# Weight and token sums of a seven-product MLP, made ahead and kept in DRAM

## The chip, the cores and the metric

The kernel runs on one core of a Trainium2 chip. The metric is the device time of one execution in microseconds, as a median of several executions. All data is float32. Each large matrix product is made of three TensorE passes over a high and a low part of both operands (below).

## What is computed

One decoder layer over 2048 tokens of width 1024: a mixer (retention heads beside pooling), cross-attention into 256 memory tokens, and a gated MLP, each with a residual, then a last RMSNorm. The change concerns the MLP, with D_FF = 2816:

```python
def conv_glu_ffn(h, w_up, conv_w, conv_b, w_down):
    a = h @ w_up
    ...
    c = conv_w[0] * a2 + conv_w[1] * a1 + conv_w[2] * a + conv_b
    gate, val = jnp.split(c, 2, axis=-1)
    return (jax.nn.silu(gate) * val) @ w_down
...
    for l in range(DEPTH):
        ...
        x = x + cross_attn(rmsnorm(x, xa_norm_g[l]), mem_n, xa_wq[l], xa_wkv[l], xa_wo[l])
        x = x + conv_glu_ffn(rmsnorm(x, ffn_norm_g[l]), ffn_w_up[l], ...)
    return rmsnorm(x, final_norm_g)
```

## The kernel before

Tokens lie along the free axis, features on the 128 partitions. The tokens are worked in two blocks of 1024 (index `b`), each of two halves of 512. A product of two float32 matrices is taken as high x high + high x low + low x high in a rounded format: `passes` (lines 227 to 229) issues the three matmuls of a weight tile and a token tile. The high part is a ScalarE copy, the low part a subtraction, mostly on VectorE (`low`, L894 and L202).

The program runs in stages. First the attention weights are folded together (`folded_weights`), beside loading of x; then, for each token block, values, four retention heads, four pooling groups, the mixed output with its residual, attention, and its output with the residual. All of these but the attention scores and the values are made of `unit`s: one weight tile of 512 KB, split into parts, against eight token tiles, 48 matmuls. Weights wait in `raws` (five places of 1024 columns in the tile R), split pairs in `prs` (three places in Q).

Then comes the MLP, for both blocks: two rounds of the up-projection (one for each block), then three rounds of the down-projection for block 0 and three for block 1. A round keeps one set of split token tiles in G, 7 x n tiles of 128 x 512, and takes its members against them. A member is a 2 x 2 block of weight tiles with a 2 x 2 block of token tiles, multiplied in seven products instead of eight (a scheme of sums, products and sums after). `Up` has n = 4 pairs per product, 22 members a block; `Down` has n = 3, 4 and 4, four members a round. Item i of a member is one product: 3n matmuls into one PSUM bank, followed by its evacuation on VectorE or ScalarE. For items 1, 2 and 5 the weight operand is a sum of tiles, which `Member.add` makes on GpSimd each time (four additions a member: the R<-R rows of GpSimd). For indices 1 to 4 the token operand is a difference, which `combining` makes on GpSimd (T<-T) from two loaded tiles of Hd (normalized tokens) or Gd (gated products). The letters in `how` say who makes the low part of each of the seven weight operands: "" is VectorE directly, "copy" ScalarE into PSUM and then VectorE, "pool" GpSimd.

Between two rounds the token tiles must be replaced in place: tile (i, j) of the next round can be written once the last member of this round has passed item i, and is wanted when the next round reaches it.

`run` writes the order of the MLP out by hand, item by item, with small queues (`pending`, `later`, `after`) for work that comes some items later. What it emits, and all of the stages before, then goes through the Tile scheduler, which simulates the engines and, on each, issues what is ready, earlier program rows first. Each engine and SP's queue of DMA issues carries out its own list in order on the chip.

Of the kernel before, what the change touches and what calls it, by code (L numbers as in the profile page):

```python
# [30 lines left out]
EDGE = 16  # L31

# [85 lines left out]
def trunk(ctx, tc, xT, memT, pos, w_qkgu, w_v, wkv, wqT, wo, wout_r, wout_p, poolT, w_up, w_dn, vecs, consts, outT):  # L118
# [55 lines left out]
    Hd = drp.tile([NB, KT, P, T], F32, tag="Hd", name="Hd")  # L174
    Gd = drp.tile([NB, NF, P, T], F32, tag="Gd", name="Gd")
# [87 lines left out]
    behind = [iter(())]  # L263
# [5 lines left out]
    def unit(raw, rhs, evac, order=range(4)):  # L269
# [4 lines left out]
        for h in range(2):  # L274
            for s in range(NS):
# [4 lines left out]
                next(behind[0], None)  # L280
                if h == 1:
                    evac(s, ps[s])
# [517 lines left out]
    def attention(sums, beside):  # L800
# [37 lines left out]
        for i in range(2 * KT):  # L838
# [22 lines left out]
            late = prob[hp], t, e  # L861
            next(more_m if i < KT - 2 else beside, None)
# [5 lines left out]


# [6 lines left out]
    class Round:  # L876


        def __init__(self, src, first, second, groups):
            self.src, self.first, self.second, self.groups = src, first, second, groups  # L880

            self.shared = False
            self.n = len(first)
            self.held = [None] * self.n
# [13 lines left out]
    def combining(rd, i, j):  # L898

        k1, k2 = rd.first[j], rd.second[j]  # L900
        r = q = None

        def load(k, s):
            r = TT.take()
            sp.dma_start(r.f[:, :SUB], rd.src(k, s))
            return r

        if i in (0, 5, 6):
            r = load(k1 if i == 0 else k2, 1 if i == 5 else 0)
        elif i in (1, 4):  # L910
            r = load(k1, 1)
            q = load(k2 if i == 1 else k1, 1 if i == 1 else 0)
        else:
            q = load(k1 if i == 2 else k2, 0)
        yield
        yield
        if i in (2, 3):
            r = rd.held[j]
        x = r.f[:, :SUB]
        if q is not None:  # L920
            a, b = (q, r) if i == 2 else (r, q)
            tt(pool, x, a.f[:, :SUB], b.f[:, :SUB], ALU.subtract)
            q.free()
            if i == 1:
                rd.held[j] = r
            yield
        hi, lo = right(i, j, 0), right(i, j, 1)
        act.activation(hi, x, AF.Copy)  # L928
        yield
        low(x, hi, lo, "pool" if rd.shared and (i * rd.n + j) % 3 == 2 else "copy" if i in (1, 2) else "")  # L930
        if i not in (1, 2):
            r.free()

    def in_turn(gens):

        live, gens = [], list(gens)
        while live or gens:
            if gens and TT.room() >= 2:
                live.append(gens.pop(0))
# [5 lines left out]
    class Member:  # L945


        def __init__(self, loads, halves):
            self.loads, self.n = loads, halves

            self.sign, self.how = 1, ("", "copy", "copy", "", "copy", "copy", "")
            self.raw = {}

        def fetch(self):

            g, h = ((0, 0), (1, 0), (1, 1), (0, 1))[len(self.raw)]
            w = self.n * P
            r = raws.take()
            sp.dma_start(r.f[:, :w], self.loads[g][:, h * w : (h + 1) * w])
            self.raw[g, h] = r  # L960

        def add(self, i):

            while len(self.raw) < (1, 2, 3, 3, 3, 4, 4)[i]:
                fetches.pop(0).fetch()
            w = self.n * P
            q = {k: r.f[:, :w] for k, r in self.raw.items()}
            a11, a12, a21, a22 = (q.get(k) for k in ((0, 0), (0, 1), (1, 0), (1, 1)))
            self.t = None
            if i == 1:  # L970
                self.t = H.take()
                x = self.t.f[:, :w]
                tt(pool, x, *((a11, a21) if self.sign > 0 else (a21, a11)), ALU.subtract)
            elif i == 2:

                tt(pool, a21, a21, a22, ALU.add)
# [670 lines left out]
```

## Time and profile before

| what | value |
|---|---|
| median of three executions | 2580.94 us (2580.14 to 2583.87) |
| profiled execution: its own time | 2577.88 us |
| profiled execution: its span | 2576.1 us |
| TensorE busy | 2468.0 us (96%) |
| VectorE / ScalarE / GpSimd busy | 1861.0 / 1246.6 / 816.4 us |
| DMA, mean over the span | 126 GB/s, 323.74 MB |

The time outside the span is 1.8 us in the profiled execution. In the span the stages before the MLP take about 1190 us, the two up-projection rounds until about 2060, the six down-projection rounds until about 2530, and the last norm the rest. A row of a group view gives line, engine, operation, output and input tiles with shapes, count, total busy time, mean of one, and the idle time before it with what ended it. One line number can be that of a helper: L202 is every two-operand operation of VectorE or GpSimd, so rows are told apart by tiles: G<-... and Q<-... are low parts of token and weight operands, Z<-... evacuations and convolution, R<-R weight sums, T<-T token sums.

### The profile page before, as it was taken

The page shows a single profiled execution, that of the slowest core. Times are in us where ns is not written, and L with a number is a line of the kernel's source. Part 1 is how long each engine was busy: PE and PEld are TensorE (multiplying, and loading weights), DVE is VectorE, ACT ScalarE, POOL GpSimd, SP SyncE. Part 2 cuts the span into 40 slices and gives each one's busy share as a digit, 9 for nine tenths or more (in the row PEclk, how much of TensorE's full clock was granted, in tenths as well). Part 3 has the DMA queues.
Part 4 walks back from the last instruction along what each step waited for, and adds up shares of the span by engine and source line. Part 5 has one row for each costly group of instructions (what it writes and reads, how often), then busy time and mean ns, then how long its engine had stood idle before and what let it go on. Part 6 is the DMA issues. An engine that isn't in the chain of part 4 may idle for free. (4 is left out here: it accounts for less than half of the span.)

```text
span 2576.1 us, 32736 instructions
## 1 busy us (share of the span) xinstructions
PE 2468.0 (96%) x11382; PEld 2045.6 (79%) x11382; DVE 1861.0 (72%) x2840; ACT 1246.6 (48%) x2240; POOL 816.4 (32%) x642
## 2 busy tenths in 40 slices
PE   7999999999999999998999999899999988989896
PEld 7888888888788888876788888688888866777675
DVE  8655564746736655435998888888888788888997
ACT  7334323534222234335555566555656574565654
POOL 0011130000301100014444445844444654543661
PEclk9999999999999999998999999899999999999998
DMA  8134424324311143144342223422222355548751
GB/s 289 49 101 141 132 83 150 115 90 141 137 33 41 35 142 119 40 169 155 106 160 98 86 94 131 147 82 86 84 89 90 136 179 184 188 165 266 252 168 70
DMA packets 166165, 323.74 MB, mean 126 GB/s; under 512 B 16752, under 2 KB 38896, under 8 KB 166000
## 3 DMA queue, kind: packets, MB, share of 16 engines
q1 hardware_dynamic: 140912, 292.29, 33.3%
q10 hardware_dynamic: 25088, 29.37, 3.3%
q8 instruction: 90, 1.47, 0.2%
q14 instruction: 75, 0.61, 0.1%
HBM read 249.76 MB, written 71.83 MB: 125 GB/s over the span
## 5 line engine op out<-in xcount | busy, mean ns | idle before, releaser
L227 PE MATMUL mm<-G,Q 128*128 128x512 f32 (+1 forms) x1944 | 755.8, 389 | 18.0 <-ACT Q L219 10.2
L228 PE MATMUL mm<-G,Q 128*128 128x512 f32 (+1 forms) x1944 | 750.1, 386 | 7.9 <-DVE G L202 7.9
L229 PE MATMUL mm<-G,Q 128*128 128x512 f32 (+1 forms) x1944 | 750.4, 386 | 7.0 <-DVE Q L202 6.9
L202 POOL TENSOR_TENSOR R<-R 128x512 f32<-128x512 f32 (+1 forms) x272 | 414.3, 1525 | 481.9 <-DMA R<-w_up 177.8
L227 PE MATMUL mm<-G 128*128 128x512 f32 (+1 forms) x1384 | 537.6, 389 | 20.4 <-DVE T L202 7.5
L228 PE MATMUL mm<-G 128*128 128x512 f32 (+1 forms) x1384 | 538.6, 389 | 16.4 <-DVE G L202 16.4
L229 PE MATMUL mm<-G 128*128 128x512 f32 (+1 forms) x1384 | 536.8, 388 | 0.0
L227 PEld LDWEIGHTS mm<-G,Q 128*128 128x128 f32 x1944 | 369.9, 190 | 91.3 <-ACT Q L219 10.6
L229 PEld LDWEIGHTS mm<-G,Q 128*128 128x128 f32 x1944 | 369.4, 190 | 82.2 <-DVE Q L202 9.6
L228 PEld LDWEIGHTS mm<-G,Q 128*128 128x128 f32 x1944 | 370.2, 190 | 80.0 <-DVE G L202 9.9
L227 PEld LDWEIGHTS mm<-G 128*128 128x128 f32 x1384 | 263.3, 190 | 77.6 <-DVE T L202 7.9
L228 PEld LDWEIGHTS mm<-G 128*128 128x128 f32 x1384 | 263.0, 190 | 75.0 <-DVE G L202 23.0
L229 PEld LDWEIGHTS mm<-G 128*128 128x128 f32 x1384 | 263.1, 190 | 52.1
L211 DVE SCALAR_TENSOR_TENSOR Z<-Z,vecs 128x1024 f32<-128x1024 f32 x176 | 254.0, 1443 | 69.8 <-ACT Z L1064 69.0
L202 DVE TENSOR_TENSOR Q<-R,Q 128x512 fp32r<-128x512 f32 (+1 forms) x234 | 175.8, 753 | 172.4 <-ACT Q L219 148.7
L202 POOL TENSOR_TENSOR T<-T 128x512 f32<-128x512 f32 (+3 forms) x140 | 203.7, 1465 | 279.3 <-PE mm L229 181.0
L202 DVE TENSOR_TENSOR Z<-Z,mm 128x512 f32<-128x512 f32 (+1 forms) x272 | 213.7, 786 | 28.7 <-PE mm L229 23.8
L894 ACT ACTIVATE aux<-R 128x512 f32<-128x512 f32 (+1 forms) x272 | 153.0, 580 | 152.6 <-POOL R L202 116.7
L202 POOL TENSOR_TENSOR Z<-Z,T 128x512 f32<-128x512 f32 x37 | 57.5, 1558 | 485.6 <-DVE T L202 398.1
L219 ACT ACTIVATE Q<-R 128x512 fp32r<-128x512 f32 x150 | 93.9, 628 | 237.1 <-PE mm L228 212.2
L928 ACT ACTIVATE G<-T 128x512 fp32r<-128x512 f32 x210 | 129.3, 628 | 155.7 <-POOL T L202 118.2
L202 DVE TENSOR_TENSOR G<-T,G 128x512 fp32r<-128x512 f32 (+1 forms) x211 | 173.2, 830 | 38.9 <-ACT G L219 18.7
(163 smaller groups left out, 2846.1 us busy)
## 6 DMA issues: line engine op xcount, KB each, us to landing
T<-Gd SPq DMA_DIRECT2D x198, 256.0 KB, 3.3
R<-w_up SPq DMA_DIRECT2D x176, 256.0 KB, 2.8
Gd<-Z SPq DMA_DIRECT2D x44, 512.0 KB, 2.6
T<-Hd SPq DMA_DIRECT2D x72, 256.0 KB, 3.1
R<-w_qkgu SPq DMA_DIRECT2D x32, 512.0 KB, 3.5
R<-w_dn SPq DMA_DIRECT2D x64, 256.0 KB, 3.3
T<-xT SPq DMA_DIRECT2D x48, 256.0 KB, 3.0
T<-Xd SPq DMA_DIRECT2D x48, 256.0 KB, 3.4
```

The costliest lines, as they stand in the source:

```text
L202: return eng.tensor_tensor(out=out, in0=a, in1=b, op=op)
L211: dve.scalar_tensor_tensor(out=out, in0=a, scalar=s, in1=b, op0=op0, op1=op1)
L219: act.activation(hi, src, AF.Copy)
L227: pe.matmul(ps, lh, rh, start=start, stop=False)
L228: pe.matmul(ps, lh, rl, start=False, stop=False)
L229: pe.matmul(ps, ll, rh, start=False, stop=stop)
L894: act.activation(t, x, AF.Copy)
L928: act.activation(hi, x, AF.Copy)
```

## The change

Four things are changed together.

Weights: a generator `weight_sums` makes, once for both blocks, the four sums of each member's weights (22 jobs for up, 12 for down) and keeps them in DRAM (`Ud`, `Dd`). It is stepped from `unit` and from the attention loop, and uses 2048 columns of R that `raws` gives up (three places instead of five). A member of the MLP then loads seven tiles instead of four and adds nothing.

Tokens: Hd and Gd hold ready-made operands, seven or eight per pair of tiles. Those of the normalized tokens are made where they are normalized (`normed_tiles`, `later_tiles`), those of the products when the second tile of a pair is done (`pair`: the first is loaded back, four GpSimd operations, four stores). `combining` loads one tile for each operand.

Low parts: `how` changes; for `Up` items 2 and 6 are GpSimd's and item 5 goes straight to VectorE; for `Down` items 2 and 6 are GpSimd's, 0, 1, 3 and 4 copied. Of the token low parts GpSimd does every third in rounds 1 and 2 as before, and now every fourth in the other rounds (`shared`).

The scheduler uses its detailed simulation (a timeline) in place of its usual one.

```diff
+ROUNDS = ((0, 3), (6, 4), (14, 4))
...
-    Hd = drp.tile([NB, KT, P, T], F32, tag="Hd", name="Hd")
-    Gd = drp.tile([NB, NF, P, T], F32, tag="Gd", name="Gd")
+    Hd = drp.tile([NB, KT // 2, 7, P, SUB], F32, tag="Hd", name="Hd")
+    Gd = drp.tile([NB, NF // 2, 8, P, SUB], F32, tag="Gd", name="Gd")
+    Ud = drp.tile([NF, 4, P, SUB], F32, tag="Ud", name="Ud")
+    Dd = drp.tile([len(ROUNDS), KT // 2, 4, P, SUB], F32, tag="Dd", name="Dd")
...
                 next(behind[0], None)
+                next(under[0], None)
...
+    def weight_sums(spare):
+        jobs = [((w_up[f], w_up[f + NF]), 0, 4, Ud[f], 1) for f in range(NF)]
+        for at, (k0, n) in enumerate(ROUNDS):
+            jobs += [((w_dn[2 * j], w_dn[2 * j + 1]), k0, n, Dd[at, j], -1) for j in range(KT // 2)]
+        for w, k0, n, to, sign in jobs:
+            q = [spare.take() for _ in range(4)]
+            a11, a12, a21, a22 = (r.f[:, : n * P] for r in q)
+            for i, a in enumerate((a11, a12, a21, a22)):
+                sp.dma_start(a, block(w, i // 2, i % 2, k0, n))
+            yield
+            yield
+            tt(pool, a22, a21, a22, ALU.add)
+            tt(pool, a21, *((a11, a21) if sign > 0 else (a21, a11)), ALU.subtract)
+            yield
+            tt(pool, a11, a22, a11, ALU.subtract)
+            tt(pool, a12, a12, a11, ALU.subtract)
+            yield
+            for i, a in enumerate((a21, a11, a22, a12)):
+                sp.dma_start(to[i][:, : n * P], a)
+            for r in q:
+                r.free()
+            yield
...
-        if q is not None:
-            a, b = (q, r) if i == 2 else (r, q)
-            tt(pool, x, a.f[:, :SUB], b.f[:, :SUB], ALU.subtract)
...
-        low(x, hi, lo, "pool" if rd.shared and (i * rd.n + j) % 3 == 2 else "copy" if i in (1, 2) else "")
+        low(x, hi, lo, "pool" if (i * rd.n + j) % rd.shared == rd.shared - 1 else "copy" if i in (1, 2) else "")
...
+    def sums_of(b11, b12, b21, b22, t):
+        tt(pool, t, b12, b22, ALU.subtract)
+        tt(pool, b12, b12, b11, ALU.subtract)
+        yield
+        tt(pool, b11, b11, t, ALU.subtract)
+        tt(pool, b21, b11, b21, ALU.subtract)
+        yield
...
+            own = [sums[i][:, : halves * P] for i in range(4)]
+            self.loads = [part(0, 0), own[0], own[1], part(1, 1), own[2], own[3], part(0, 1)]
...
-            self.b, self.f, self.how = b, f, ("", "copy", "copy", "", "copy", "copy", "pool")
+            self.b, self.f, self.how = b, f, ("", "copy", "pool", "", "copy", "", "pool")
...
+                def pair():
+                    if TT.room() < 3:
+                        after(1, pair)
+                        return
+                    x = [TT.take() for _ in range(3)]
+                    b11, b12, t = (r.f[:, :SUB] for r in x)
+                    sp.dma_start(b12, to[7])
+                    sp.dma_start(b11, to[0])
+                    todo = sums_of(b11, b12, one, two, t)
...
-            self.b, self.j, self.at, self.sign = b, j, at, -1
+            self.b, self.j, self.at, self.how = b, j, at, ("copy", "copy", "pool", "copy", "copy", "", "pool")
...
-        out[1].shared = out[2].shared = True
+        out[1].shared = out[2].shared = 3
...
+    raws = Places([(R, j * T) for j in range(3)], T)
+    under[0] = weight_sums(Places([(R, 3 * T + i * SUB) for i in range(4)], SUB))
...
-    with tile.TileContext(nc) as tc:
+    with tile.TileContext(nc, schedule_with_timeline_sim=True) as tc:
```

Where the order moves: SP's queue in the front, from the loads of the positions (`pos`) on. w_qkgu are the weights of the heads' units, wqT those of a folding step; w_up into R and R into Ud are the sums' loads and stores. Before:

```order
L531 DMA T<-pos 64x512 x2
L286 DMA R<-w_qkgu 128x1024 x2
L403 DMA R<-wqT 128x1024 x2
L286 DMA R<-w_qkgu 128x1024
L403 DMA R<-wqT 128x1024
L286 DMA R<-w_qkgu 128x1024 x2
```

and now, from the same loads:

```order
L536 DMA T<-pos 64x512 x2
L291 DMA R<-w_qkgu 128x1024
L408 DMA R<-wqT 128x1024
L889 DMA R<-w_up 128x512 x2
L899 DMA Ud<-R 128x512 x2
L889 DMA R<-w_up 128x512 x2
L899 DMA Ud<-R 128x512
L889 DMA R<-w_up 128x512 x2
L408 DMA R<-wqT 128x1024
L899 DMA Ud<-R 128x512 x3
```

The second wqT now stands behind six loads and three stores of sums, and the scheduler has drawn the jobs far ahead of the places where the program steps them: the loads of the last of the 34 stand before the sixth wout_r load of block 0. SP issues 1569 transfers in all, where it issued 953.

GpSimd's queue near the end of the down-projection. R<-R are weight sums, T<-T token sums; G<-R,G and G<-T,G are low parts of weight and token operands. Before:

```order
L202 TENSOR_TENSOR T<-T 128x512 x5
L202 TENSOR_TENSOR R<-R 128x512
L202 TENSOR_TENSOR T<-T 128x512
L202 TENSOR_TENSOR R<-R 128x512
L202 TENSOR_TENSOR T<-T 128x512 x4
```

and now:

```order
L206 TENSOR_TENSOR G<-T,G 128x512 x3
L206 TENSOR_TENSOR G<-R,G 128x512
L206 TENSOR_TENSOR G<-T,G 128x512
L206 TENSOR_TENSOR G<-R,G 128x512
L206 TENSOR_TENSOR G<-T,G 128x512
```

No sums are left on GpSimd there; what stands in their place are low parts that were VectorE's.

More of the change, by code (lines that the diff above doesn't have):

```diff
@@ L861, in attention @@
             late = prob[hp], t, e
+            next(under[0], None)
             next(more_m if i < KT - 2 else beside, None)
@@ L1257, in after, with until_room @@
         waiting.append((clock[0] + n, f))
+    def until_room(places, n):
+        for _ in range(99):
+            if places.room() >= n:
+                return
+            w = min(waiting, key=lambda w: w[0])
+            waiting.remove(w)
+            w[1]()
+        assert False, "no room"
     pending, later, sums, Y, fetches = [], [], [], [], []
@@ L1275, in run @@
         items = [(rd, g, m, i) for rd in rds for g in rd.groups for i in range(7) for m in g]
-        fetches[:] = [m for rd in rds for g in rd.groups for _ in range(4) for m in g]
-        made, added, highs = [], [], []
+        fetches[:] = [(m, i) for _, _, m, i in items]
+        made, highs = [], []
         tiles, due, live = [], [], []
@@ L1555, in trunk @@
     more()
+    for a in (state.rearrange("p h n -> p (h n)"), cs_t[:, P + 1 : P + 1 + SUB]):
+        TT.freed.append(len(TT.one))
+        TT.one.append(Arena(a, 0, 1, SUB))
     for r in xs:
```

227 lines of the change are left out of this document (112 added, 115 removed).

## The prediction

> **What bounds the kernel now.** I read the page's head, then busy time by stretches of the span, then TensorE's waits, then groups by form. The page:
>
> ```profile
> span 2576.1 us, 32736 instructions
> PE 2468.0 (96%) x11382; PEld 2045.6 (79%) x11382; DVE 1861.0 (72%) x2840; ACT 1246.6 (48%) x2240; POOL 816.4 (32%) x642
> ```
>
> The stretches; columns are stretch, length, then busy us and instructions of PE, PEld, DVE, ACT, POOL, then granted clock, DMA share, GB/s:
>
> ```profile
> 0.00:70.00 70.00, 54.50 (x402) 51.92 (x402) 61.09 (x104) 49.73 (x81) 6.29 (x9) 0.98 0.76 273
> 50.00:60.00 10.00, 6.82 (x44) 6.42 (x43) 8.96 (x13) 6.56 (x11) 0.00 (x0) 0.83 1.00 346
> 45.00:400.00 355.00, 349.19 (x1841) 299.81 (x1841) 218.47 (x434) 136.94 (x282) 45.46 (x42) 1.00 0.36 115
> 650.00:1175.00 525.00, 520.25 (x2489) 434.37 (x2489) 276.56 (x580) 152.43 (x332) 66.32 (x57) 1.00 0.26 89
> 1175.00:1275.00 100.00, 85.22 (x353) 67.77 (x352) 79.23 (x107) 54.43 (x91) 47.76 (x35) 0.91 0.38 128
> 1300.00:1600.00 300.00, 300.00 (x1326) 248.47 (x1325) 257.85 (x300) 178.45 (x279) 142.46 (x112) 1.00 0.31 109
> 1620.00:1680.00 60.00, 50.22 (x191) 39.10 (x190) 53.65 (x54) 35.18 (x59) 48.01 (x35) 0.89 0.40 133
> 2060.00:2520.00 460.00, 416.92 (x1747) 334.43 (x1746) 404.69 (x546) 278.89 (x516) 242.44 (x173) 0.96 0.59 197
> ```
>
> TensorE is the bound almost everywhere: in the middle of the first up-projection round it is busy 300 of 300 us and issues 1326 matmuls, 4.42 per us or 0.226 us each. Nothing done for the other engines there can pay. Counting matmuls against that rate shows where time is lost, the lowered clock included: entry to the up-projection (1175 to 1275) 353 of 442, so 89 / 4.42 = 20 us; change of token block (1620 to 1680) 191 of 265, 17 us; down-projection (2060 to 2520) 1747 of 2033, 65 us. The prize is at most these 102 us. Before them, 650 to 1175 loses under 5 us.
>
> Who is waited for there: TensorE's waits at the block change (first row) and from 2000 on (the others); columns are total us, times, longest.
>
> ```profile
> PE mm L228 <- DVE G L202: 8.1, 5, 2.4
> ...
> PE mm L228 <- DVE G L202: 16.3, 12, 4.1
> PE aux L296 <- DVE T L202: 12.3, 2, 9.9
> PE mm L227 <- DVE Z L202: 10.0, 9, 2.0
> ```
>
> G is the token operand, Z the accumulators: VectorE's low parts and evacuations come last. Beside them VectorE is busy 405 of 460 us (88%) in the down-projection. Its groups, then GpSimd's, from 2080 to 2510 (count | busy, mean ns | idle before):
>
> ```profile
> L202 DVE TENSOR_TENSOR G<-T,G 128x512 fp32r<-128x512 f32 x102 | 90.0, 896 | 5.7 <-ACT G L928 5.3
> L202 DVE TENSOR_TENSOR G<-aux,G 128x512 fp32r<-128x512 f32 x73 | 48.3, 682 | 9.8 <-ACT aux L894 5.6 <-ACT G L989 3.4
> L202 DVE TENSOR_TENSOR Q<-R,Q 128x512 fp32r<-128x512 f32 x23 | 19.3, 838 | 7.3 <-ACT Q L989 7.3
> L202 DVE TENSOR_TENSOR G<-R,G 128x512 fp32r<-128x512 f32 x21 | 19.2, 915 | 6.4 <-ACT G L989 6.3
> L202 DVE TENSOR_TENSOR G<-R,G 128x384 fp32r<-128x384 f32 x12 | 9.4, 779 | 0.5 <-ACT G L989 0.5
> L202 DVE TENSOR_TENSOR Q<-R,Q 128x384 fp32r<-128x384 f32 x10 | 6.6, 657 | 1.6 <-ACT Q L989 1.6
> ...
> L202 POOL TENSOR_TENSOR T<-T 128x512 f32<-128x512 f32 x76 | 109.2, 1450 | 55.5 <-DMA T<-Gd 43.7 <-ACT aux L894 6.9 <-issue 4.2
> L202 POOL TENSOR_TENSOR R<-R 128x512 f32<-128x512 f32 x62 | 91.0, 1472 | 105.5 <-DMA R<-w_dn 66.9 <-DVE Q L202 27.3 <-issue 6.9
> L202 POOL TENSOR_TENSOR R<-R 128x384 f32<-128x384 f32 x24 | 28.3, 1185 | 43.2 <-DMA R<-w_dn 21.4 <-DVE Q L202 8.6 <-issue 5.7
> ```
>
> The sums that the change takes away here are GpSimd's R and T rows. What helps VectorE is that GpSimd, freed of them, takes over low parts.
>
> **Down-projection, by steps.** A member is one pair of weight tiles. Its seven low parts were three direct VectorE ones and four through a ScalarE copy; now two are GpSimd's, one direct, four copied. Over 24 members VectorE loses 48 direct ones; the four R rows give (19.3 + 19.2 + 9.4 + 6.6) / 66 = 0.83 us, so 40 us. Of 154 token tiles GpSimd did 7 low parts (every third of one round of 21) and will do 40 (one round at every third, five at every fourth): 33 fewer, 5 in 7 at 0.90 and 2 in 7 at 0.68, so 28 us. GpSimd's stretch falls from 242 us to 32 x 1.47 + 16 x 1.19 + 40 x 1.47 = 125. The gap of 0.21 us between 896 and 682, which only operations with both inputs in SBUF show, should then halve: on some 170 such operations 17 us more. VectorE goes from 405 to about 320 us, while the 1747 matmuls need 395: 81%. In the steady up-projection it stands at 258 of 300, 86%, and TensorE loses nothing. So load ceases to be the limit; bursts at round changes and the 9.9 us wait of the statistics remain. I take 35 of the 65 us, with 10 and 60 as ends.
>
> On that gap the Trainium skill (SBUF — State Buffer, section Who interferes with whom) states an exclusive lock: with two SBUF inputs VectorE is fully blocked for as long as GpSimd's reading instruction holds the pair. By it an operation arriving at random against 53% occupancy by 1.45 us would wait 0.38 us, not the 0.21 shown, and the halving would be worth about 31 us instead of 17; the sum uses the row.
>
> **The two entries.** One token tile at the up-projection's start, engine by engine, in the timeline (start, length, instruction, idle before):
>
> ```profile
> 1198.21 1.29 POOL L202 TENSOR_TENSOR T<-T 128x512 f32<-128x512 f32 x1 [3.23 <-DMA T<-Hd]
> 1199.53 0.63 ACT L928 ACTIVATE G<-T 128x512 fp32r<-128x512 f32 x1 [1.81 <-POOL T L202]
> 1200.20 1.10 DVE L202 TENSOR_TENSOR G<-T,G 128x512 fp32r<-128x512 f32 x1 [2.22 <-ACT G L928]
> ...
> 1215.29 0.79 PE L227 MATMUL mm<-G 128*128 128x512 f32 x1 [7.51 <-DVE T L202]
> ```
>
> The tile arrives ready-made now: GpSimd's 1.3 us and the second load go, while ScalarE's and VectorE's steps stay. I take half of each loss: 10 (2 to 16) and 8 (0 to 14) us. At the block change GpSimd was 80% busy (48 of 60), which is the load removed.
>
> **Up-projection between them: nothing.** ScalarE loses 88 copies, VectorE 44 low parts. GpSimd loses 176 sums, gains 44 low parts and 88 sums of product tiles: per second-half tile 2 x 1.47 + 4 x 1.45 = 8.7 us and two short halo copies, of the 19 us that its 84 matmuls take. Three more loads per member ride on a DMA share of 0.31. TensorE's 300 of 300 hides all of it; were GpSimd late, seven operand buffers (19 us) stand between.
>
> **The front, where the cost lies.** The sums of 34 jobs (22 up, 12 down) each load four tiles, make four GpSimd operations and store four, all on SP's queue, among the loads TensorE lives on. SP issues 1569 transfers instead of 953; at 0.33 us that is 203 us more of a mostly idle queue. Not issuing but waiting counts: a store waits for GpSimd, a load waits until the last store from its buffer has landed, and behind these in order stand the loads of w_qkgu, wqT, wo and wout, whose buffers fall from five to three. In the new order all 34 jobs stand between the first w_v load and the sixth wout_r. SP's issues of the second w_v load and the sixth wout_r, and landing times from the list of DMA issues:
>
> ```profile
> 43.03 0.38 SPq L635 DMA_DIRECT2D Z<-w_v  x1
> ...
> 380.70 0.33 SPq L1433 DMA_DIRECT2D R<-wout_r  x1
> ...
> R<-w_up SPq DMA_DIRECT2D x176, 256.0 KB, 2.8
> Hd<-T SPq DMA_DIRECT2D x32, 256.0 KB, 2.4
> T<-Yd SPq DMA_DIRECT2D x16, 256.0 KB, 4.2
> T<-wkv SPq DMA_DIRECT2D x8, 256.0 KB, 6.7
> ```
>
> One job's loop, in the buffer that binds: two GpSimd operations, the store's landing, the load's landing: 2 x 1.47 + 2.4 + 2.8 = 8.1 us with light traffic, 2.9 + 2 x 4.2 = 11.3 with the T<-Yd landing, 2.9 + 2 x 6.7 = 16.3 with that of the start. TensorE's pace leaves (380.7 - 43.0) / 34 = 9.9 us a job. Traffic: 22 + 8 jobs of 2.1 MB and 4 of 1.57 make 69 MB, over 338 us 205 GB/s on top of 115, so 320, against 346 at a share of 1.00. That is near the limit but below it, so I put the loop at 9.6 us (landings of 3.0 and 3.7, nearer the light rows because a late job also asks for less): no drift, but now and then a weight tile that is late. I charge 5 us. At the start VectorE is busy 61 of 70 us and the first stores stand ahead of the last x loads: 4 us. At the second token block the 16 sums of the normalized tiles (16 x 1.47 = 24 us) keep their Z buffers to the end, and the values of the block want them after two units (2 x 48 matmuls x 0.226 = 22 us): 3 us. Together 12; ends 0 and 40. A gain here is bounded by the 5 us lost from 650 to 1175.
>
> The scheduler's other simulation changes the order on every queue. In the front TensorE returns to a half-done accumulation more often than before, so its operands come in later by that simulation; no row prices it, and the ends just given, minus 5 to plus 40, hold it.
>
> **The sum.** -35 - 10 - 8 + 12 = -41 us. Profiled execution: 2577.88 us, with 2576.1 of span; to 2536.9. The median is 2580.94, 3.06 above that execution, so I predict 2540 us. About 0.2%, 5 us, is what a measurement of this kernel can tell from no change.
>
> **Rivals.**
>
> *The front becomes SP's.* If landings under the doubled traffic reach the T<-Yd row and beyond, the loop outgrows 9.9 us, and every job shifts all weight loads behind it. Two units of prefetch, 22 us, cover the first drift. At 13 us a job: 34 x 3.1 - 22 = 83 us, in place of the 12: 2540 - 12 + 83 = 2611. With the start's landing, 16.3: 34 x 6.4 - 22 = 196, so 2724. The change turns into a loss where the front costs 53 us, at (53 + 22) / 34 + 9.9 = 12.1 us a job. For it: 320 of 346 GB/s. Against: the loop slows itself, and light landings leave 1.8 us. Chance 0.25.
> The Trainium skill (DMA: Bandwidth & Descriptors, section Latency and other measured facts) says the same of HBM: 0.2 us of access on average, 2 us under high load. With 1.8 us more on both landings the loop would be an estimated 11.7 us and the front would cost 39; the rows here show 2.8 growing to 6.7 in the start.
>
> *The down-projection stays late by its handoffs.* The 9.9 us statistics wait, lowered clock and GpSimd's 1.47 us low parts (against 0.83) could keep bursts as they are. With 10 in place of 35: 2565. For it: waits are short and many (12 for 16.3 us). Against: 88% of VectorE. Chance 0.13.
>
> *Nearly all of the loss goes.* 60 + 10 + 8 with a free front: 2503. Chance 0.06.
>
> That the sums are not moved at all is excluded: the order has all of them in the front.
>
> **How the numbers follow.** Forecast 0.56, front 0.25, handoffs 0.13, all 0.06. Forecast's own range, from the mixed ends of its terms: 2515 to 2565. Faster by over 0.2%: 0.56 + 0.06 + 0.10 of the handoffs = 0.72; within: 0.04; slower: 0.24. The range 2508 to 2600 leaves out the larger part of the front's case and half of the best.
>
> **What would show it.** Right: TensorE stays busy from 45 to 400 us, and the sums run from the first to the last job in about 340 us; down-projection near 425 us for the same matmuls, VectorE near 80%, GpSimd near 125 us; waits for G less than half. Wrong: TensorE waiting in the front for Q or G behind DMA into R, with SP's queue full of Ud stores; 13 us between one job's store and the next; VectorE still above 86% in the down-projection; or a new wait for GpSimd's low parts.

## The result, and the profile after

The changed kernel takes 2583.61 us (median of 20 runs), the kernel before 2580.84 (20 runs); the ratio is 1.0009, with a 95% interval of 0.9999 to 1.0018. No change can be told, where 2540 us and a gain had been forecast. The profiled execution took 2586.36 us, with a span of 2584.1.

The page of the kernel after: TensorE's share is what it was, ScalarE and GpSimd do a little less.

```profile
span 2584.1 us, 33903 instructions
PE 2469.4 (96%) x11382; PEld 2053.7 (79%) x11382; DVE 1863.9 (72%) x2708; ACT 1191.3 (46%) x2138; POOL 803.2 (31%) x638
```

Busy time by stretches of the kernel after (columns as in the prediction). The windows of the entry, the block change and the down-projection are moved so that they hold the same places of the program:

```profile
45.00:400.00 355.00, 319.78 (x1649) 273.78 (x1650) 235.21 (x361) 116.84 (x251) 181.15 (x131) 0.94 0.77 253
650.00:1175.00 525.00, 509.91 (x2425) 425.74 (x2424) 307.60 (x590) 155.72 (x336) 71.13 (x58) 0.98 0.27 89
1248.00:1348.00 100.00, 100.00 (x450) 82.96 (x450) 73.47 (x105) 56.88 (x90) 21.34 (x19) 1.00 0.50 156
1300.00:1600.00 300.00, 294.26 (x1301) 242.26 (x1300) 256.67 (x295) 155.05 (x233) 142.54 (x106) 1.00 0.62 200
1687.00:1747.00 60.00, 57.51 (x254) 47.19 (x253) 55.42 (x61) 34.22 (x55) 35.37 (x29) 1.00 0.64 209
2114.00:2574.00 460.00, 440.15 (x1924) 360.35 (x1922) 381.65 (x531) 294.60 (x537) 132.87 (x97) 0.98 0.66 220
```

The MLP got what was forecast for it, and more: the entry holds 450 matmuls in 100 us instead of 353, the block change 254 in 60 instead of 191, the down-projection 1924 in 460 instead of 1747. The steady up-projection, where nothing was forecast, has 1301 in 300 us instead of 1326. The front gave the gain back: 1649 matmuls from 45 to 400 us instead of 1841, TensorE busy for 320 of 355 us instead of 349, at a granted clock of 0.94 instead of 1.00.

Four events cut the span into stages: the first softmax exponential of each token block's attention (ScalarE's rows for the line of the exponential, with first and last start), the first eviction of the up-projection and the first of the down-projection (the timeline). Of the kernel before:

```profile
L853 ACT ACTIVATE T<-mm,sm,scl x32: 547/558/567, 475.3 to 559.6; 128x256 f32<-128x256 f32 x32
L853 ACT ACTIVATE T<-mm,sm,scl x32: 552/562/572, 1010.9 to 1096.4; 128x256 f32<-128x256 f32 x32
```
```profile
1203.50 0.59 ACT L1022 ACTIVATE Z<-mm 128x512 f32<-128x512 f32 x1
2079.32 0.57 ACT L1118 ACTIVATE Z<-mm 128x512 f32<-128x512 f32 x1
```

The same rows of the kernel after:

```profile
L858 ACT ACTIVATE T<-mm,sm,scl x32: 549/556/567, 552.4 to 632.2; 128x256 f32<-128x256 f32 x32
L858 ACT ACTIVATE T<-mm,sm,scl x32: 547/557/569, 1104.0 to 1185.1; 128x256 f32<-128x256 f32 x32
```
```profile
1276.21 0.59 ACT L1016 ACTIVATE Z<-mm 128x512 f32<-128x512 f32 x1
2133.13 1.05 ACT L1140 ACTIVATE Z<-mm 128x512 f32<-128x512 f32 x2
```

Differences between them, in us; those of the experiments, read from the same four events of their profiles, stand in the same table. "Front" is up to the first event, "second block" to the second, then the entry to the up-projection, the up-projection, and the down-projection to the end.

| kernel | front | second block | entry | up | down | span | median |
|---|---|---|---|---|---|---|---|
| before | 475.3 | 535.6 | 192.6 | 875.8 | 496.8 | 2576.1 | 2580.84 |
| **after** | 552.4 | 551.6 | 172.2 | 856.9 | 451.0 | 2584.1 | 2583.61 |
| before, detailed simulation | 488.3 | 532.7 | 182.5 | 861.0 | 476.7 | 2541.2 | 2549.86 |
| after, usual simulation | 593.9 | 554.8 | 177.1 | 859.3 | 454.9 | 2640.0 | 2645.97 |
| no weight sums | 487.7 | 548.7 | 172.7 | 857.3 | 451.3 | 2517.7 | 2519.78 |
| copies alone | 514.0 | 551.5 | 172.4 | 861.1 | 449.9 | 2548.9 | 2544.03 |
| GpSimd operations alone | 543.7 | 548.9 | 172.9 | 856.5 | 447.5 | 2569.5 | 2571.96 |
| sums on VectorE | 533.9 | 548.4 | 172.8 | 855.9 | 451.2 | 2562.2 | 2564.66 |
| GpSimd writing only (one run: 2523.61) | 553.2 | 551.4 | 172.7 | 857.5 | 449.9 | 2584.7 | 2585.28 |
| transfers on GpSimd's queue | 539.1 | 559.7 | 172.0 | 856.9 | 451.5 | 2579.2 | 2582.12 |
| paced | 510.2 | 570.7 | 172.3 | 854.3 | 449.3 | 2556.8 | 2563.73 |
| paced, token sums on VectorE | 511.2 | 554.6 | 172.3 | 856.2 | 448.1 | 2542.4 | 2547.86 |
| paced, all these on VectorE | 505.4 | 554.7 | 172.7 | 859.4 | 449.2 | 2541.4 | 2541.25 |
| down-projection's sums alone | 494.9 | 543.5 | 173.8 | 871.1 | 448.6 | 2531.9 | 2535.31 |

Each row is one profiled execution; most lie within 4 us of the median, that of the paced kernel 5 below it (2558.61), that of the kernel before with the detailed simulation 7 below (2543.08), that of the copies 7 above (2550.66).

So, before to after: +77 (front) + 16 (second block) - 20 (entry) - 19 (up) - 46 (down) = +8 us of span.

### The profile page after: what moved, and what is told of

Read it like the earlier page. It is cut to its first block, busy times and chain, and to the rows that moved or that the text cites. A ratio compares the mean times of both kernels' runs of the same rounds, so it can differ in the third digit from the quotient of the medians.

```text
span 2584.1 us, 33903 instructions
## 1 busy us (share of the span) xinstructions
PE 2469.4 (96%) x11382; PEld 2053.7 (79%) x11382; DVE 1863.9 (72%) x2708; ACT 1191.3 (46%) x2138; POOL 803.2 (31%) x638
## 4 chain that ended last, share of the span: by engine, by line
PE 72%; DMA 11%; DVE 7%; POOL 4%; issue 3%; ACT 2%; SPq 1%; DVEq 0%; POOLq 0%; ACTq 0%
PE mm L231 23%; PE mm L232 23%; PE mm L233 23%; DMA R<-w_up 3%; POOL R L206 2%; DMA Ud<-R 2%; DVE G L206 2%; DVE Z L206 1%; DVE Z L215 1%; DVE T L206 1%; DMA Gd<-T 1%; POOL T L206 1%; DMA T<-Xd 1%; DMA T<-Gd 1%; DMA VWd<-T 1%
## 5 line engine op out<-in xcount | busy, mean ns | idle before, releaser
L215 DVE SCALAR_TENSOR_TENSOR Z<-Z,vecs 128x1024 f32<-128x1024 f32 x176 | 246.5, 1403 | 50.0 <-ACT Z L1059 28.6
L206 POOL TENSOR_TENSOR R<-R 128x512 f32<-128x512 f32 (+1 forms) x136 | 193.2, 1420 | 210.7 <-DMA R<-w_up 127.7
L206 DVE TENSOR_TENSOR Q<-R,Q 128x512 fp32r<-128x512 f32 x198 | 152.3, 771 | 138.1 <-ACT Q L223 133.0
L206 POOL TENSOR_TENSOR G<-R,G 128x512 fp32r<-128x512 f32 (+1 forms) x100 | 146.1, 1464 | 321.2 <-ACT G L986 279.6
L986 ACT ACTIVATE G<-R 128x512 fp32r<-128x512 f32 (+1 forms) x272 | 163.4, 613 | 156.8 <-PE mm L232 139.4
L206 DVE TENSOR_TENSOR G<-R,G 128x512 fp32r<-128x512 f32 (+1 forms) x169 | 147.5, 884 | 58.1 <-ACT G L223 50.6
L206 POOL TENSOR_TENSOR G<-T,G 128x512 fp32r<-128x512 f32 x47 | 66.7, 1421 | 358.8 <-ACT G L938 315.8
L1059 ACT ACTIVATE Z<-Z,vecs 128x1024 f32<-128x1024 f32 x88 | 109.4, 1244 | 138.1 <-DVE Z L206 138.0
```

The lines of the kernel that those rows point to most:

```text
L206: return eng.tensor_tensor(out=out, in0=a, in1=b, op=op)
L215: dve.scalar_tensor_tensor(out=out, in0=a, scalar=s, in1=b, op0=op0, op1=op1)
L986: act.activation(p2[:, 0, :w], self.raw[i].f[:, :w], AF.Copy)
L1059: act.activation(self.c[g].f, a[:, 2:], AF.Identity, bias=cb[:, f : f + 1], scale=cw[2][:, f : f + 1])
```

## The experiments

The theories: the front lost its time (T) to the order that the detailed simulation made, (Q) to the jobs' transfers, in SP's queue or in memory, or (G) to GpSimd's operations, which hold VectorE back. Theory S of the first expectations stands for the sums themselves, whether by Q, by G or by the three raw buffers.

### Which part of the change costs

**The change with the usual simulation.**

```diff
-    with tile.TileContext(nc, schedule_with_timeline_sim=True) as tc:
+    with tile.TileContext(nc) as tc:
```

> The kernel after with the scheduler's usual simulation; all else as changed. In the kernel after, the first token block's attention starts 78 us later than before and the whole front gives away some 75 to 90 us, while the MLP gains about 82. Theory S (the weight sums cost the front, by their transfers in SP's queue, by GpSimd's work beside VectorE, or by the three raw buffers): the simulation matters little, time within 10 us of the kernel after's 2584 us, first attention step still near 548 us. Theory T (the detailed simulation puts the sums' transfers at bad places): time falls by 40 us or more, to 2540 or below, first attention step back towards 470 us. A rise by more than 10 us would say that the simulation hides a part of the loss.

2645.97 us, ratio to before 1.025 (1.0232 to 1.0269): the rise that the expectation named last. The simulation doesn't cause the loss, it hides part of it: without it the front takes 119 us more than before, not 77.

**The kernel before with the detailed simulation alone.**

```diff
-    with tile.TileContext(nc) as tc:
+    with tile.TileContext(nc, schedule_with_timeline_sim=True) as tc:
```

> The kernel before with the detailed simulation alone. Theory T: the front loses here too, 40 us or more, so 2620 us or above. Theory S: within 10 us of 2581. A gain of some 5 to 10 us in the MLP from a better order alone would also show here, as a shorter stretch from the first up-projection eviction to the end (1373 us before).

2549.86 us, ratio 0.9881 (0.9864 to 0.9898): both theories missed. One word in the call, and the kernel before gains 31 us. Its entry and its down-projection, in the windows of the kernel before:

```profile
1175.00:1275.00 100.00, 91.86 (x400) 75.04 (x399) 86.43 (x109) 59.85 (x98) 50.86 (x37) 0.97 0.40 132
2060.00:2520.00 460.00, 429.49 (x1852) 347.39 (x1850) 419.79 (x569) 289.62 (x529) 248.05 (x169) 0.98 0.59 193
```

400 matmuls instead of 353, and 1852 instead of 1747: of the 89 and 286 matmuls by which these windows fall short of the steady rate, 47 and 105 were lost to order, not to load. The program's work for VectorE and GpSimd is the same, and VectorE's share of the down-projection even rises, to 91%. In the front this order costs 13 us. The two parts of the change thus overlap: in the MLP (entry, up and down) the rest of the change gains 74 us under the usual simulation, but only 40 beyond what the detailed one gives by itself.

**The change without the weight sums.** The 34 jobs are gone and the MLP loads unsummed tiles in place of the sums, so its output is another; all else stays. This holds for the next three kernels too.

```diff
-            own = [sums[i][:, : halves * P] for i in range(4)]
+            own = [part(1, 0), part(0, 0), part(1, 1), part(0, 1)]
...
-    under[0] = weight_sums(Places([(R, 3 * T + i * SUB) for i in range(4)], SUB))
```

> The kernel after without the sums of the weights: the 34 jobs are left out, and the MLP loads unsummed weight tiles in their place (as many bytes, the output is another). Three raw buffers, token sums and simulation stay. Theory S with the cause in the jobs themselves: the front is as before (first attention step near 470 us) and the MLP keeps its gain, so 2581 - 82 = about 2500 us. If the three raw buffers are the cause: the front keeps most of its loss, above 2550. If the simulation is: the same, above 2550. Between 2510 and 2545: the jobs share the loss with one of these.

2519.78 us, ratio 0.9766 (0.9748 to 0.9783): 20 us above the first answer, and inside the range (2510 to 2545) that the expectation kept for a loss that the jobs share. The front (487.7) is that of the kernel before with the detailed simulation (488.3): there three raw buffers cost nothing, and the jobs share the front's loss with the simulation's 13 us alone. The second block's 16 us stay (548.7 against 532.7), so they are not the jobs' either. The jobs cost the remaining 64 us of the median, all of it in the front (552.4 against 487.7).

### Transfers or GpSimd

From that kernel, one half of the jobs was put back at a time. **Copies alone:** the four loads and four stores of each job without the four operations between them.

```diff
-            tt(pool, a22, a21, a22, ALU.add)
-            tt(pool, a21, *((a11, a21) if sign > 0 else (a21, a11)), ALU.subtract)
             yield
-            tt(pool, a11, a22, a11, ALU.subtract)
-            tt(pool, a12, a12, a11, ALU.subtract)
```

> The kernel without weight sums in the MLP, but with the jobs' loads and stores in the front as copies, without their four GpSimd operations (the MLP takes unsummed tiles; the output is another). Against the same kernel without jobs (2520 us): theory Q gives the transfers at least 40 of the 65 us, so 2560 or above; a job's loop without GpSimd is shorter, so the copies also come faster and crowd the weight loads more. Theory G: 2520 to 2535.

2544.03 us, 24 above the kernel without jobs and between the two answers. ScalarE, which makes the high parts of the weights, now waits for weight tiles (its waits from 80 to 470 us; total, times, longest); in the kernel without jobs no row for w_qkgu stands there, and wqT has 1.4 us.

```profile
ACT Q L223 <- DMA R<-w_qkgu: 30.0, 4, 10.5
ACT G L223 <- DMA R<-wqT: 20.5, 3, 13.3
```

The kernel after has the same two rows at the same size, so this is what the transfers do there too:

```profile
ACT Q L223 <- DMA R<-w_qkgu: 30.8, 5, 10.0
ACT G L223 <- DMA R<-wqT: 21.1, 3, 12.0
```

**GpSimd's operations alone:** no loads and no stores; the buffers are filled once and the 136 operations work on them.

```diff
-            q = [spare.take() for _ in range(4)]
+        q = [spare.take() for _ in range(4)]
+        for r in q:
+            dve.memset(r.f, 1.0)
...
-            for i, a in enumerate((a11, a12, a21, a22)):
-                sp.dma_start(a, block(w, i // 2, i % 2, k0, n))
...
-            for i, a in enumerate((a21, a11, a22, a12)):
-                sp.dma_start(to[i][:, : n * P], a)
```

> The kernel without weight sums in the MLP, but with the 136 GpSimd operations of the jobs in the front, on constant data in the same four buffers, without loads and stores (the MLP takes unsummed tiles; the output is another). Against the same kernel without jobs (2520 us): theory G gives them 40 us or more, 2560 or above, with VectorE's low parts near 0.94 us; theory Q 2520 to 2535. Both this and the copies near 2550 would share the cost between the two.

2571.96 us, 52 above the kernel without jobs, as theory G had it: the larger share, 56 us of front against the copies' 26. Both together cost 64, less than the 82 of the two runs; how they overlap, no run took apart. VectorE's groups from 80 to 470 us (count | busy, mean ns | idle before), first without jobs:

```profile
L206 DVE TENSOR_TENSOR G<-R,G 128x512 fp32r<-128x512 f32 x45 | 31.5, 729 | 33.4 <-ACT G L223 29.6 <-PE mm L233 3.7
L206 DVE TENSOR_TENSOR Q<-R,Q 128x512 fp32r<-128x512 f32 x49 | 34.1, 697 | 50.2 <-ACT Q L223 49.9
L206 DVE TENSOR_TENSOR T<-mm,Z 64x512 f32<-64x512 f32 x32 | 22.0, 688 | 0.6
L215 DVE SCALAR_TENSOR_TENSOR sm<-sm,sm 128x4 f32<-128x4 f32 x48 | 9.5, 199 | 1.4
```

With GpSimd's operations alone, and GpSimd's own row last:

```profile
L206 DVE TENSOR_TENSOR G<-R,G 128x512 fp32r<-128x512 f32 x41 | 48.8, 1226 | 18.3 <-ACT G L223 18.3
L206 DVE TENSOR_TENSOR Q<-R,Q 128x512 fp32r<-128x512 f32 x39 | 35.9, 919 | 29.1 <-ACT Q L223 28.8
L206 DVE TENSOR_TENSOR T<-mm,Z 64x512 f32<-64x512 f32 x32 | 22.0, 688 | 0.6
L215 DVE SCALAR_TENSOR_TENSOR sm<-sm,sm 128x4 f32<-128x4 f32 x48 | 20.4, 425 | 1.4
...
L206 POOL TENSOR_TENSOR R<-R 128x512 f32<-128x512 f32 x115 | 169.8, 1485 | 6.3
```

Operations with both inputs in SBUF go from 0.73 and 0.70 us to 1.23 and 0.92; even those of four columns go from 0.20 to 0.43. The one with an input in PSUM (mm) stays at 688 ns to the nanosecond. Waiting in GpSimd's own queue isn't the cause here: from 60 to 560 us the other engines wait 2.9 us for GpSimd's results, against 2.7 without jobs. The kernel after shows the same longer operations in its front:

```profile
L206 DVE TENSOR_TENSOR G<-R,G 128x512 fp32r<-128x512 f32 x41 | 40.0, 1003 | 47.5 <-ACT G L223 46.6 <-PE mm L233 0.9
L206 DVE TENSOR_TENSOR Q<-R,Q 128x512 fp32r<-128x512 f32 x37 | 36.1, 978 | 40.6 <-ACT Q L223 40.5
L206 DVE TENSOR_TENSOR T<-mm,Z 64x512 f32<-64x512 f32 x32 | 21.9, 688 | 0.6
L215 DVE SCALAR_TENSOR_TENSOR sm<-sm,sm 128x4 f32<-128x4 f32 x48 | 20.1, 419 | 1.4
```

TensorE's two longest waits of its front (60 to 520 us; total, times, longest), neither of which the kernel without jobs has, are one for the last of such a chain of VectorE operations (T) and one for GpSimd's own Z results, which come out of the same queue as the sums:

```profile
PE aux L760 <- DVE T L206: 14.4, 5, 3.7
PE aux L721 <- POOL Z L206: 13.0, 3, 7.3
```

The first is there at 15.2 us with GpSimd's operations alone; the second is not, so in the kernel after GpSimd's queue has a part of its own.

**GpSimd writing only:** each operation as two memsets.

```diff
-            tt(pool, a22, a21, a22, ALU.add)
+            pool.memset(a22, 1.0)
+            pool.memset(a22, 1.0)
```
(and so for the other three)

> As the kernel with the jobs' GpSimd operations alone (2572 us), but each of the 136 operations is two memsets of the same tile, which write and read nothing (again no transfers, and the MLP takes unsummed tiles; the output is another). If VectorE was held back by GpSimd's reading, its operations with both inputs in SBUF go back from 1.2 to 0.7 us and the time to that without jobs, 2520 to 2530. If GpSimd's queue was the cause (the rotary sums of q and k standing behind the jobs), or any GpSimd work beside VectorE, the time stays above 2545, as long as the memsets keep GpSimd busy for a similar time.

Of ten runs nine took 2579 to 2588 us and one 2523.61, within 4 us of no jobs at all. The profile is of one of the nine. VectorE from 80 to 470 us, then TensorE's timeline (start, length, idle before):

```profile
L210 DVE TENSOR_SCALAR T<-T,consts 128x512 f32<-128x512 int32 x1 | 59.9, 59850 | 0.0
L206 DVE TENSOR_TENSOR G<-R,G 128x512 fp32r<-128x512 f32 x41 | 29.1, 736 | 31.3 <-ACT G L223 30.5 <-PE mm L233 0.6
```
```profile
149.07 0.79 PE L232 MATMUL mm<-G 128*128 128x512 f32 x1 [54.63 <-DVE G L206]
```

The group's mean is back at 0.74 us, but most of these operations ran beside an idle GpSimd: its memsets lie before 70 us, from 79 to 148 and from 210 to 239 us. What counts are the operations in those stretches. VectorE's timeline, then GpSimd's:

```profile
216.41 0.69 DVE L206 TENSOR_TENSOR G<-R,G 128x512 fp32r<-128x512 f32 x1 [2.19 <-ACT G L223]
228.98 2.10 DVE L206 TENSOR_TENSOR G<-R,G 128x512 fp32r<-128x512 f32 x2 [0.20 <-ACT G L223]
231.85 0.69 DVE L206 TENSOR_TENSOR G<-R,G 128x512 fp32r<-128x512 f32 x1 [0.78 <-ACT G L223]
```
```profile
216.26 0.42 POOL L899 MEMSET R<- 128x384 f32 x1
228.13 1.79 POOL L206 TENSOR_TENSOR Z<-Z,T 128x512 f32<-128x512 f32 x1
231.73 0.53 POOL L898 MEMSET R<- 128x512 f32 x1
```

Beside a memset a low part takes 0.69 us; the one pair that meets a GpSimd operation which reads takes 2.10 instead of 1.38. So theory G holds in its form "GpSimd's reading". The time of the nine runs is an accident of another kind, seen in the profiled one: a single TENSOR_SCALAR took 59.85 us (0.48 in the kernel without jobs) while 129 memsets started on GpSimd, one every 0.47 us without a gap, and TensorE waited 54.6 us behind it. 2586.5 - 54.6 = 2532, near the one run that, by its time, escaped it. That the other eight met the same is argued from their times.

The Trainium skill (SBUF — State Buffer, section Who interferes with whom) states just this pair of rules: a VectorE instruction with two SBUF inputs contends with a GpSimd instruction that reads SBUF and not with one that only writes, and a tensor_scalar can enter a two-port mode, in which it contends as well. These runs agree with both. That the loser was passed over for 129 instructions in a row is more than the page says.

### Other places for the same work

**The four operations on VectorE.**

```diff
-            tt(pool, a22, a21, a22, ALU.add)
+            tt(dve, a22, a21, a22, ALU.add)
```
(and so for the other three)

> The kernel after with the four operations of each weight sum on VectorE, not on GpSimd. VectorE then has 136 operations more in the front, at about 0.7 us some 95 us more work in the 390 us in which it is 62% busy: 86%. Theory G (GpSimd's reading holds VectorE back: VectorE's low parts there grew from 0.70 to 0.94 us): they fall to about 0.7 us again and the front's loss of some 80 us shrinks to 20 to 40; total 2525 to 2545. Theory Q (the transfers in SP's queue, each waiting for the sums or for a buffer, hold up the weight tiles behind them): the loop of a job loses 2 x (1.46 - 0.7) = 1.5 us of 10.8, at most 34 x 1.5 = 50 us, but VectorE's own queue delays the sums, so the front keeps at least half its loss; total 2555 to 2600, and SP's waits for the sums stand with VectorE's name in place of GpSimd's.

2564.66 us, ratio 0.9938 (0.9923 to 0.9953), 19 less than the kernel after. The low parts fell to 0.71 and 0.74 us as theory G has it, but the time lies in theory Q's range, and 46 of the 64 us in the front remained: VectorE now has the operations themselves (95 us of work), and the transfers stay. How the 46 divide between these two, no run took apart.

**The jobs' transfers on GpSimd's queue.**

```diff
-                sp.dma_start(a, block(w, i // 2, i % 2, k0, n))
+                pool.dma_start(a, block(w, i // 2, i % 2, k0, n))
...
-                sp.dma_start(to[i][:, : n * P], a)
+                pool.dma_start(to[i][:, : n * P], a)
```

> The kernel after with the jobs' loads and stores issued from GpSimd's queue instead of SP's. If SP's order is what counts (weight loads standing behind a store that waits for GpSimd or a load that waits for a buffer), the front's loss falls to 30 us or less: 2530 to 2550. If it is the traffic itself or GpSimd's work beside VectorE, it stays: 2570 to 2600; issuing takes GpSimd time of its own, which can also make it slower.

2582.12 us, 1.0002 (0.9991 to 1.0014): 13 us less in the front, 8 more in the second block, as the second answer had it. So taking the transfers out of SP's queue is worth little on balance. What it is worth by itself the run doesn't show, since each of the 272 issues now takes GpSimd 0.55 us, 151 us in all.

**Paced jobs.** The program hands the jobs out over both blocks, but the scheduler let all 34 run ahead, as fast as buffers came free. SP's timeline of the kernel after, first and last load of a job (the 72 and 430 us of the expectation were both misread):

```profile
34.05 0.33 SPq L889 DMA_DIRECT2D R<-w_up  x1
...
464.66 0.33 SPq L889 DMA_DIRECT2D R<-w_dn  x1
```

Here each job's loads stand behind the latest load of a weight tile.

```diff
-        sp.dma_start(raw, src.rearrange("p k n -> p (k n)"))
+        anchor[0] = sp.dma_start(raw, src.rearrange("p k n -> p (k n)"))
...
+            with tc.issue_after(anchor[0].ins):
                 for i, a in enumerate((a11, a12, a21, a22)):
                     sp.dma_start(a, block(w, i // 2, i % 2, k0, n))
             yield
             yield
+            yield
```

> The kernel after with the four loads of each weight sum ordered, on SP's queue, behind the latest load of a weight tile that the program has written by then, and one step more per job: the jobs are spread over both token blocks (about 24 in the first, 10 in the second) instead of all running ahead from 72 to 430 us. Theory Q (weight tiles late because the sums run ahead and fill queue and memory): the 65 us that the sums cost the front fall to 25 or less, total 2520 to 2545. Theory G (GpSimd's presence beside VectorE): the same number of operations costs about the same wherever it lies, total 2570 or above.

2563.73 us, 0.9929 (0.9914 to 0.9944): 20 less, between the two answers. The front's 64 us fall to 22, and 19 come back in the second block, where 15 of the 34 jobs now lie.

**And the first block's token sums on VectorE.** In the kernel without jobs TensorE stands still in the second block's start while GpSimd makes those 16 sums, among other operations (stretch; then TensorE's timeline):

```profile
700.00:720.00 20.00, 4.41 (x17) 3.28 (x16) 16.48 (x13) 0.63 (x1) 20.00 (x16) 0.63 0.42 159
```
```profile
718.50 0.80 PE L231 MATMUL mm<-G 128*128 128x512 f32 x1 [15.59 <-DVE T L206]
```

GpSimd is busy 20 of 20 us, and VectorE needs 16.48 us for 13 instructions.

```diff
-            sp.dma_start(raw[:, SUB:], WPd[n].rearrange("p k c -> p (k c)"))
+            anchor[0] = sp.dma_start(raw[:, SUB:], WPd[n].rearrange("p k c -> p (k c)"))
...
-            todo = sums_of(*q, t.f[:, :SUB])
+            todo = sums_of(*q, t.f[:, :SUB], pool if b + 1 == NB else dve)
```

> As the paced kernel (2564 us), with two changes: the loads of wout_r and its partner also hold back the jobs that follow, and the 16 sums of the first block's normalized tokens are VectorE's. In the kernels with token sums TensorE waits once for 15.6 us at the second block's values while GpSimd is busy 20 of 20 us, and the stretch from the first block's attention to the second's is 16 us longer. If that is GpSimd's 16 sums, it falls by 10 to 16, and the pacing of the wout stage gives 5 to 10: 2540 to 2550. If not: 2555 to 2565.

2547.86 us, 0.9883 (0.9867 to 0.9899): 16 less than the paced kernel, all in the second block; what holding the jobs of the wout stage back gave was not measured by itself. But the wait that the expectation named is still there. TensorE's, from 600 to 1200 us, first in the paced kernel, then here:

```profile
PE mm L231 <- DVE T L206: 14.6, 2, 9.5
```
```profile
PE mm L231 <- DVE T L206: 14.2, 2, 8.4
```

And the stage, at 554.6 us, is 3 above that of the kernel after and 22 above that of the simulation alone (532.7). So the move won back about what the paced jobs had added there (19 us), not the 16 that the change costs without any jobs.

**The weight sums on VectorE as well.**

> As the run before with the weight sums on VectorE as well, spread over both blocks: 136 operations of about 0.7 us, 95 us of VectorE over 1100 us in which it is some 57% busy. If GpSimd's reading is the main cost and the transfers when spread cost less than the 26 us of the bunched copies, 2515 to 2535, below the 2550 of the kernel before with the detailed simulation alone. If VectorE's added work delays the operands as much as GpSimd's did: 2545 or above.

2541.25 us, 0.9853 (0.9837 to 0.987): below both kernels, and between the two answers, 6 us above the range of the first. Its ratio is under that of the detailed simulation alone (0.9881), but the two intervals overlap.

**The down-projection's sums alone.** As the run before, but only 12 jobs are left; the up-projection loads four raw tiles, sums in place on GpSimd, and has its low parts made by the same engines as in the kernel before.

```diff
-        jobs = [((w_up[f], w_up[f + NF]), 0, 4, Ud[f], 1) for f in range(NF)]
+        jobs = []
...
+            if i == 1:
+                tt(pool, self.t.f[:, :SUB], a11, a21, ALU.subtract)
+            elif i == 2:
+                tt(pool, a21, a21, a22, ALU.add)
+                tt(pool, a11, a21, a11, ALU.subtract)
+            elif i == 5:
+                tt(pool, a11, a12, a11, ALU.subtract)
```

> As the paced kernel with the sums on VectorE (2541 us), but only the down-projection's 12 jobs are made ahead (one per 16 steps); the up-projection loads its four raw tiles and sums them in place on GpSimd, in each token block, as the kernel before does. By the stages, the change took 26 us off the down-projection and only 4 off the up-projection beyond what the simulation alone gave, while 22 of the 34 jobs are the up-projection's. If so, the front and the second block win back two thirds of the 24 us that the paced jobs still cost there, and the up-projection gives back 4: 2525 to 2535. If the up-projection or the entry needs the ready-made sums, they lose 10 to 20: 2545 or above.

2535.31 us, 0.983 (0.9817 to 0.9843), 45.6 less than before and the best of the kernels that compute the layer. The front and the second block win 22 us back over the run before; the up-projection gives 12, not 4. Its GpSimd is busy 214 of 300 us, against 142 before and 143 in the kernel after:

```profile
1300.00:1600.00 300.00, 286.05 (x1240) 234.10 (x1239) 267.30 (x283) 164.29 (x254) 214.36 (x148) 0.99 0.46 154
```

Whether that is GpSimd's reading once more, or the order of the loads, no run took apart.

## Why the prediction was wrong

**The step that failed is the front's term, "Together 12; ends 0 and 40".** It measured 77 + 16 = 93 us. It was priced from SP's queue alone: issues, landings, a loop of 9.6 us a job. The loop came out at (464.7 - 34.1) / 34 = 12.7, but that is not what the loss hangs on (see the rivals). What was not priced at all is the 136 GpSimd operations beside VectorE. The prediction had the fact in hand, the gap between 896 and 682 ns, and booked its shrinking as a gain in the down-projection, but no cost in the front, where GpSimd went from 45 to 181 us of 355. Of the 77, the simulation has 13; of the other 64, GpSimd's operations make 56 alone and the transfers 26 alone. That the total is only 44 us off is luck: the MLP gained 85 us where 53 were forecast, and the loss ahead of it was 93 where 12 were.

**"3 us" for the normalized tiles' sums** at the second block was sized by how long they hold buffers. The stage lost 16. Every kernel in the table with token sums, three raw buffers and the new stores in that stage spends 543 us or more there, the two without them 536 or less, and at its start TensorE waits 13 to 16 us for VectorE in the kernel after, without jobs and in the paced ones. With the sums on VectorE this wait stayed. So which of these parts makes it stays open.

**The simulation** had no row, as the prediction said, and its ends were put into the front only. Alone it is worth -31 us of the median: by the stages +13 in the front, -3 in the second block and -45 in the MLP. Why the rest of the change costs the front 119 us under the usual simulation and 64 under the detailed one is open; no run took that apart.

**The MLP's terms** had the right sign and were too small: 46 for 35, 20 and 19 for 10 and 8. But only 26, 10 and 4 of these are there beyond what the simulation gives by itself. The step about VectorE was half wrong. These are the low parts of the tokens in the kernel after, 2134 to 2564 us, and those of the weights that GpSimd took over:

```profile
L206 DVE TENSOR_TENSOR G<-T,G 128x512 fp32r<-128x512 f32 x62 | 56.0, 916 | 7.1 <-ACT G L938 7.1
```
```profile
L206 POOL TENSOR_TENSOR G<-R,G 128x512 fp32r<-128x512 f32 x32 | 44.3, 1386 | 122.1 <-ACT G L986 114.2 <-DMA state<-Gd 3.9 <-DMA T<-Gd 3.9
```

GpSimd's time fell to 133 us (125 forecast), yet the operations are at 916 ns, not nearer to 682: the gap's 17 us never came, and no run shows why. VectorE stands at 382 of 460 us, 83%, with 10% more matmuls served. The simulation alone gave 20 of the 46 us without taking work from VectorE; how the other 26 divide between less load and fewer handoffs, no run took apart. TensorE's waits for VectorE's G fell from 16.3 us to 0.2; its longest there (2050 us to the end) are now these:

```profile
PE aux L1240 <- DVE Q L206: 5.1, 2, 3.3
PE mm L231 <- DVE Z L206: 5.0, 3, 2.9
```

**The rivals.** "The front becomes SP's" named the size, 83 us, the 13 us a job (12.7 measured, for which its formula gives 34 x 2.8 - 22 = 73 us), and the signs to look for (late w_qkgu tiles, Ud stores in the queue), and they are there. But the long loop goes along with the loss more than it makes it. With the copies alone a job takes (374.9 - 33.5) / 34 = 10.0 us, for which the formula gives nothing, and they cost 24; GpSimd's operations cost 52 without a transfer; and with the transfers in GpSimd's queue, where no weight load stands behind a job, the whole costs the same (GpSimd pays for the issues there). The size was right in part by luck, and the chance of 0.25 stood on the wrong price.

## What to carry to other kernels

Work put on an idle GpSimd was not free here, where VectorE has two-input SBUF operations on the path: find a pair of VectorE rows, one with a PSUM input and one without, and read the price from their difference before moving work there. Work ahead that has no deadline should be tied to the transfers it must not overtake; this scheduler, seeing a free buffer, ran it at once. And measure the parts of a change apart: here one word of it gained 31 us alone, the rest lost them, and together they looked like nothing.

## What the runs showed of the hardware

A VectorE operation of 128x4 elements went from 0.199 to 0.425 us beside GpSimd's reading, 0.23 more, where two groups of 128x512 lost 0.22 and 0.50: the loss is not in proportion to VectorE's elements. With an input in PSUM, 688 ns stayed 688, and beside a memset a low part took 0.69. And one VectorE TENSOR_SCALAR of 0.48 us stood for 59.85 us against an unbroken row of 129 GpSimd memsets; by their times, nine runs of ten met this.
